# Top-10 indices of 8192 rows: the end of the kernel overlapped by hand, and one tile's loads divided by partitions

## The chip, the cores and the metric

One core of a Trainium2 chip. The metric is the device time of one execution in microseconds; a kernel's number is the median of its fast runs. How ratios are computed: the mean time of one kernel's fast runs over the mean of the other's fast runs of the same rounds, which is not quite the ratio of the medians quoted beside it.

## The reference

```python
def setup_inputs():
    return {"x": np.random.randn(8192, 8192).astype(np.float32), "k": 10}

def reference(x, k):
    indices = np.argpartition(x, -k, axis=1)[:, -k:]
    values = np.take_along_axis(x, indices, axis=1)
    sorted_idx = np.argsort(-values, axis=1)
    return np.take_along_axis(indices, sorted_idx, axis=1)
```

## The kernel before

The 268 MB of x pass the core once, in 64 tiles of 128 rows (4.2 MB each). A tile goes through these stages: SP issues its loads (four pieces); ScalarE takes exp(36(x - 4.7)) in bf16; PE sums groups of these with a 0/1 matrix, so that large elements stand out (1024 sums per row group, 512 for the last three "thin" tiles); VectorE chooses the 12 largest sums and their indices; GpSimd (POOL) gathers the candidates from the tile; VectorE and POOL spread them by a mask; PE extracts them; VectorE ranks them. Every eight tiles or so a batch is finished and written. At the end a check decides whether a slow fallback must run.

```python
    def load(t):
        lay = layout(t)
        xts[t] = xpool.tile([P, N], fp32, tag="xt", name="xt")          # 4 buffers
        src = x[t * P:(t + 1) * P, :].rearrange("(s a) (q j) -> (a q) s j", a=lay.A, q=lay.R)
        dst = xts[t].rearrange("p (s j) -> p s j", j=lay.W)
        n = lay.S // (8 if t in (0, last) else 4)
        for s in range(0, lay.S, n):
            nc.sync.dma_start(out=dst[:, s:s + n, :], in_=src[:, s:s + n, :])
    ...                                                # (cut)
    with tc.manual_schedule():
        weigh(0)
        later = []
        for t in range(last):
            interleave(choose_steps(t), rank_steps(t - LAG) if t >= LAG else [])
            if t >= 1:
                spread(t - 1)
            gather(t)
            weigh(t + 1)
            ...                                        # (cut: extract, steps of a finished batch)
            if t + 3 < ntiles:
                load(t + 3)
        extract(last - 3)
        extract(last - 2)
        run(choose_steps(last))
        spread(last - 1)
        gather(last)
        extract(last - 1)
        ...                                            # (cut: check, rankings, two batches)
```

## Time and profile before

| | before |
|---|---|
| median time | 683.44 us (682.9 to 683.74, 3 runs) |
| span of the profiled run | 679.8 us |
| transfer rate in the loop | about 420 GB/s |
| VectorE, PE, ScalarE, POOL busy | 82%, 81%, 72%, 26% |

The way to read it: the DMA share is 9 tenths in 38 of 40 slices, so the kernel is bound by them, and what a change of the end can win lies behind the last landing. The prediction below shows the lines and reads them.

### The profile page before, as it was taken

How to read it: one execution, taken by the hardware profiler on the slowest of the kernel's cores; microseconds unless marked ns; L12 is line 12 of the kernel's file. 1: busy time of each engine (PE TensorE's matmuls, PEld its weight loads, DVE VectorE, ACT ScalarE, POOL GpSimd, SP SyncE). 2: the span in 40 equal slices, each digit the busy share in tenths (PEclk: the TensorE clock that was granted, in tenths of full speed). 3: DMA queues.
4: the chain of work that ended last, by engine and by line, in shares of the span. 5: the costliest groups of instructions: out<-in, count | busy, mean ns of one | idle time of the engine just before them, and what ended most of it. 6: DMA issues, size and time to landing. Idle time of an engine off the chain costs nothing.

```text
span 679.8 us, 7988 instructions
## 1 busy us (share of the span) xinstructions
PE 549.6 (81%) x2690; PEld 339.5 (50%) x2690; DVE 555.5 (82%) x1335; ACT 488.7 (72%) x264; POOL 178.9 (26%) x134
## 2 busy tenths in 40 slices
PE   1577777888887889887987898898888789887887
PEld 0144544554544565553753555655454355454566
DVE  2577878699779978789796998879977889879687
ACT  4777777777777777777777777777777777777740
POOL 0113133313322322313322313322332231331330
PEclk9887887687878768597686768767788768778786
DMA  9999999999999999999999999999999999999910
GB/s 351 420 421 420 422 418 419 421 419 421 420 420 420 421 419 420 421 419 421 420 421 419 421 419 422 418 420 421 419 421 419 421 419 419 420 420 392 385 39 7
DMA packets 73696, 269.77 MB, mean 397 GB/s; under 512 B 4382, under 2 KB 5046, under 8 KB 73654
## 3 DMA queue, kind: packets, MB, share of 16 engines
q1 hardware_dynamic: 72960, 268.54, 96.8%
q10 hardware_dynamic: 694, 0.71, 0.3%
q8 instruction: 21, 0.34, 0.2%
q14 instruction: 21, 0.17, 0.1%
HBM read 268.58 MB, written 0.66 MB: 396 GB/s over the span
## 4 chain that ended last, share of the span: by engine, by line
DMA 62%; PE 10%; DVE 8%; SPq 6%; ACT 5%; issue 4%; POOL 3%; ACTq 0%; DVEq 0%
DMA xt<-in_x_dram 62%; PE s L169 8%; SPq L101 6%; ACT e L162 5%; POOL cand L203 3%; PE g L233 2%; DVE wall L189 2%; DVE m L190 1%; DVE masked L221 1%; DVE cidb L194 0%; DVE cidb L192 0%; DVE wall L193 0%; DVE rows L301 0%; DVE g L246 0%; DVE pick L298 0%
## 5 line engine op out<-in xcount | busy, mean ns | idle before, releaser
L162 ACT ACTIVATE e<-xt,bias 128x4096 bf16<-128x4096 f32 (+2 forms) x131 | 475.5, 3630 | 155.4 <-DMA xt<-in_x_dram 143.2
L169 PE MATMUL s<-e,group 128*128 128x512 bf16 x1024 | 337.5, 491 | 123.7 <-ACT e L162 123.4
L169 PEld LDWEIGHTS <-group 128*128 128x128 bf16 x1024 | 121.7, 122 | 316.3 <-issue 259.4
L233 PEld LDWEIGHTS g<-cpack,masked 128*128 128x128 f32 x1536 | 206.4, 214 | 16.5 <-issue 5.4
L233 PE MATMUL g<-cpack,masked 128*128 128x8 f32 (+1 forms) x1536 | 199.1, 269 | 1.7 <-DVE masked L221 1.7
L203 POOL INDIRECT_COPY cand<-xt,idx 128x192 f32 x64 | 64.9, 1014 | 478.8 <-DMA xt<-in_x_dram 181.8
L189 DVE MAX8 wall<-s 128x8 f32<-128x1024 f32 (+1 forms) x64 | 77.2, 1206 | 116.2 <-PE s L169 116.1
L221 POOL TENSOR_TENSOR masked<-cand,cpack 128x768 f32<-128x768 f32 x63 | 113.1, 1795 | 5.3
L192 DVE FIND_INDEX8 cidb<-wall,s 128x8 uint16<-128x1024 f32 (+1 forms) x64 | 76.6, 1197 | 0.0
L194 DVE FIND_INDEX8 cidb<-wall,m 128x8 uint16<-128x1024 f32 (+1 forms) x64 | 76.3, 1193 | 0.0
L190 DVE MATCH_REPLACE8 m<-wall,s 128x1024 f32<-128x1024 f32 (+1 forms) x64 | 76.0, 1188 | 0.0
L193 DVE MAX8 wall<-m 128x8 f32<-128x1024 f32 (+1 forms) x64 | 75.6, 1181 | 0.0
L221 DVE TENSOR_TENSOR masked<-cand,cpack 128x768 f32<-128x768 f32 x64 | 61.4, 960 | 0.9 <-POOL cand L203 0.9
L281 PE MATMUL fo<-rows,send 128*64 128x160 f32 (+3 forms) x128 | 27.9, 369 | 1.1 <-DVE rows L301 1.1
L162 ACT ACTIVATION_READ_ACCUMULATOR e<-xt,bias 128x1 f32 x131 | 24.4, 186 | 0.0
L281 PEld LDWEIGHTS fo<-rows,send 128*64 128x64 f32 (+2 forms) x128 | 18.3, 159 | 3.5 <-DVE rows L301 1.6
L248 DVE FIND_INDEX8 posb<-t8a,g 128x8 uint16<-128x96 f32 (+1 forms) x64 | 16.6, 260 | 0.0
L250 DVE FIND_INDEX8 posb<-t8b,g 128x8 uint16<-128x96 f32 (+1 forms) x64 | 16.4, 255 | 0.0
L245 DVE MAX8 t8a<-g 128x8 f32<-128x96 f32 (+1 forms) x64 | 16.1, 252 | 0.0
L246 DVE MATCH_REPLACE8 g<-t8a,g 128x96 f32<-128x96 f32 (+1 forms) x64 | 16.1, 251 | 0.0
L249 DVE MAX8 t8b<-g 128x8 f32<-128x96 f32 (+1 forms) x64 | 15.8, 246 | 0.0
L362 ACT ACTIVATE e<-tall,bias 128x64 f32<-128x64 f32 x1 | 0.3, 347 | 19.6 <-DVE tall L251 19.6
(37 smaller groups left out, 105.7 us busy)
## 6 DMA issues: line engine op xcount, KB each, us to landing
xt<-in_x_dram SPq DMA_DIRECT2D x248, 1024.0 KB, 16.3
xt<-in_x_dram SPq DMA_DIRECT2D x16, 512.0 KB, 9.4
out_dram<-opack ACTq DMA_DIRECT2D x6, 80.0 KB, 5.2
cpack<-topk_cpack ACTq DMA_DIRECT2D x1, 141.0 KB, 3.3
out_dram<-opack ACTq DMA_DIRECT2D x1, 70.0 KB
out_dram<-opack SPq DMA_DIRECT2D x1, 60.0 KB, 1.9
out_dram<-opack SPq DMA_DIRECT2D x1, 30.0 KB, 1.5
```

What stands on the lines that cost most here:

```text
L101: nc.sync.dma_start(out=dst[:, s:s + n, :], in_=src[:, s:s + n, :])
L162: nc.scalar.activation(out=e[:, 0:n * W], in_=xts[t][:, s0 * W:(s0 + n) * W], func=ACTF.Exp, bias=bias[:, 0:1], scale=BETA, accum_out=eall ...
L169: nc.tensor.matmul(ss[t][:, j:j + BANK], lhsT=lay.group[:, s0 + i, :], rhs=e[:, i * W + j:i * W + j + BANK], start=s0 + i == 0, stop=s0 + ...
L189: lambda: nc.vector.max(out=w16[:, 0:8], in_=m),
L190: lambda: nc.vector.match_replace(out=m2, in_to_replace=w16[:, 0:8], in_values=m, imm_value=-1.0),
L192: lambda: nc.vector.max_index(out=cid[:, 0:8], in_max=w16[:, 0:8], in_values=m),
L193: lambda: nc.vector.max(out=w16[:, 8:16], in_=m2),
L194: lambda: nc.vector.max_index(out=cid[:, 8:16], in_max=w16[:, 8:16], in_values=m2),
L203: nc.gpsimd.add_instruction(mybir.InstIndirectCopy(name=nc.get_next_instruction_name(), ins=[nc.gpsimd.lower_ap(xts[t]), nc.gpsimd.lower_a ...
L221: eng.tensor_tensor(out=masked[t][:, g0:g1], in0=cand[:, g0:g1].unsqueeze(2).to_broadcast(shape), in1=layout(t).own.rearrange("p (c s) -> ...
L233: nc.tensor.matmul(gs[t][:, c * R:(c + 1) * R], lhsT=mk[:, c, :, :].rearrange("p a s -> p (a s)"), rhs=layout(t).place, start=True, stop=True)
L281: nc.tensor.matmul(fo, lhsT=lay.send[:, i, 0:n * S], rhs=rows[:, i].rearrange("p a k -> p (a k)"), start=i == 0, stop=i == n - 1)
```

## The change

Two intents. The first is to overlap the last three tiles by hand: finer pieces for ScalarE and PE, the last two gathers in two halves, work of one tile put between the steps of another, some work of the last but one batch moved from VectorE to ScalarE. The second is to divide the loads of tile 61 by partitions, so that the DMA engines thought to run late get less. (Late: of the 16 semaphore increments that the trace of before shows for a load, one comes 2.5 to 2.9 us after the next in the last dozen loads. That one, or the DMA engine behind it, is called the straggler.) The pad is meant to keep the tiles' addresses at the same place modulo 512 bytes.

```diff
-PAD = 208
+PAD = 320
+
+DIVIDED = [[120, P], [120, 124, P], [112, P], [104, P]]
...
-        n = lay.S // (8 if t in (0, last) else 4)
-        for s in range(0, lay.S, n):
-            nc.sync.dma_start(out=dst[:, s:s + n, :], in_=src[:, s:s + n, :])
+        s = 0
+        for i, n in enumerate(pieces(t)):
+            bounds = DIVIDED[i] if t == last - 2 else [P]
+            for p0, p1 in zip([0] + bounds, bounds):
+                nc.sync.dma_start(out=dst[p0:p1, s:s + n, :], in_=src[p0:p1, s:s + n, :])
+            s += n
...
+        a, b, c = last - 2, last - 1, last
+        run(later)
+        wb, wc = weigh_steps(b), weigh_steps(c)
+        run(wb[0:3])
+        extract(a - 1, 0, 6)
+        run(wb[3:4])
+        extract(a - 1, 6, G)
+        run(wc[0:4])
+        run(rank_steps(a - 2))
+        mask(nc.gpsimd, a, G // 2, G)
+        run(choose_steps(b))
...   (cut: the rest of the hand-made order; gather in halves; two steps on ScalarE)
```

More of the change, by code (lines that the diff above doesn't have):

```diff
@@ L92, in layout, with pieces, parts @@
         return thin if t >= ntiles - TAIL else wide
+    def pieces(t):
+        S = layout(t).S
+        if t == 0:
+            return [S // 8] * 8
+        return [S // 8] * 7 + [S // 16] * 2 if t == last else [S // 4] * 4
+    def parts(t):
+        S = layout(t).S
+        if t < ntiles - TAIL:
+            return [S // 2] * 2
+        return [S // 4] + [S // 8] * 5 + [S // 16] * 2 if t == last else [S // 4] * 4
     def load(t):
@@ L146 @@
     tall = consts.tile([P, ntiles], fp32)
-    nsums = 2 * ntiles + 3
+    first_sum = np.cumsum([0] + [len(parts(t)) for t in range(ntiles)]).tolist()
+    nsums = first_sum[-1]
     eall = consts.tile([P, nsums], fp32)
@@ L152, with weigh_steps @@
         nc.gpsimd.memset(o, 0)
-    def weigh(t):
+    def weigh_steps(t):
         lay = layout(t)
@@ L157, in weigh, with part @@
         ss[t] = spsum.tile([P, wide.W], fp32, tag="s", name="s")[:, 0:W]
-        parts = [S // 4, S // 4, S // 4, S // 8, S // 8] if t == last else [S // 2, S // 2]
-        s0 = 0
-        for h, n in enumerate(parts):
+        def part(h, s0, n):
             e = epool.tile([P, N // 2], bf16, tag="e", name="e")
@@ L164, in weigh @@
                 func=ACTF.Exp, bias=bias[:, 0:1], scale=BETA,
-                accum_out=eall[:, 2 * t + h:2 * t + h + 1],
+                accum_out=eall[:, first_sum[t] + h:first_sum[t] + h + 1],
             )
@@ L168, in weigh @@
                 for j in range(0, W, BANK):
-                    nc.tensor.matmul(ss[t][:, j:j + BANK], lhsT=lay.group[:, s0 + i, :],
+                    nc.tensor.matmul(sums[:, j:j + BANK], lhsT=lay.group[:, s0 + i, :],
                                      rhs=e[:, i * W + j:i * W + j + BANK],
                                      start=s0 + i == 0, stop=s0 + i == S - 1)
+        sums, steps, s0 = ss[t], [], 0
+        for h, n in enumerate(parts(t)):
+            steps.append(lambda h=h, s0=s0, n=n: part(h, s0, n))
             s0 += n
+        return steps
     def choose_steps(t):
@@ L187, in choose_steps, with index, gather @@
         idxs[t] = small.tile([P, G], u16, tag="idx", name="idx")
+        def index(g0, g1):
+            nc.vector.tensor_scalar(
+                out=idxs[t][:, g0:g1], in0=cid[:, g0:g1], scalar1=float(lay.W - 1),
+                scalar2=lay.base, op0=ALU.min, op1=ALU.add,
+            )
+        early = t >= last - 1
         return [
             lambda: nc.vector.max(out=w16[:, 0:8], in_=m),
+            lambda: nc.vector.max_index(out=cid[:, 0:8], in_max=w16[:, 0:8], in_values=m),
+        ] + ([lambda: index(0, G // 2), lambda: gather(t, 0, G // 2)] if early else []) + [
             lambda: nc.vector.match_replace(out=m2, in_to_replace=w16[:, 0:8], in_values=m,
                                             imm_value=-1.0),
-            lambda: nc.vector.max_index(out=cid[:, 0:8], in_max=w16[:, 0:8], in_values=m),
             lambda: nc.vector.max(out=w16[:, 8:16], in_=m2),
             lambda: nc.vector.max_index(out=cid[:, 8:16], in_max=w16[:, 8:16], in_values=m2),
-            lambda: nc.vector.tensor_scalar(
-                out=idxs[t], in0=cid[:, 0:G], scalar1=float(lay.W - 1), scalar2=lay.base,
-                op0=ALU.min, op1=ALU.add,
-            ),
-        ]
-    def gather(t):
-        cands[t] = small.tile([P, G, 16], fp32, tag="cand", name="cand")
+        ] + ([lambda: index(G // 2, G), lambda: gather(t, G // 2, G)] if early
+             else [lambda: index(0, G)])
+    def gather(t, g0, g1):
+        if g0 == 0:
+            cands[t] = small.tile([P, G, 16], fp32, tag="cand", name="cand")
         nc.gpsimd.add_instruction(
@@ L205, in gather @@
                 name=nc.get_next_instruction_name(),
-                ins=[nc.gpsimd.lower_ap(xts[t]), nc.gpsimd.lower_ap(idxs[t])],
-                outs=[nc.gpsimd.lower_ap(cands[t].rearrange("p g s -> p (g s)"))],
-                num_valid_indices=16 * G,
-            )
-        )
-        del xts[t], idxs[t]
-    def spread(t, ndve=G // 2):
-        masked[t] = small.tile([P, G, P // 16, 16], fp32, tag="masked", name="masked")
-        cand = cands.pop(t)
-        for eng, g0, g1 in ((nc.vector, 0, ndve), (nc.gpsimd, ndve, G)):
-            if g0 == g1:
-                continue
-            shape = [P, g1 - g0, P // 16, 16]
-            eng.tensor_tensor(
-                out=masked[t][:, g0:g1],
-                in0=cand[:, g0:g1].unsqueeze(2).to_broadcast(shape),
-                in1=layout(t).own.rearrange("p (c s) -> p c s", s=16).unsqueeze(1).to_broadcast(shape),
-                op=ALU.mult,
-            )
@@ L228, in extract, with mask @@
-    def extract(t):
-        mk = masked.pop(t)
-        gs[t] = gpsum.tile([P, G * thin.R], fp32, tag="g", name="g")
+                ins=[nc.gpsimd.lower_ap(xts[t]), nc.gpsimd.lower_ap(idxs[t][:, g0:g1])],
+                outs=[nc.gpsimd.lower_ap(cands[t][:, g0:g1].rearrange("p g s -> p (g s)"))],
+                num_valid_indices=16 * (g1 - g0),
+            )
+        )
+        if g1 == G:
+            del xts[t], idxs[t]
+    def mask(eng, t, g0, g1):
+        if t not in masked:
+            masked[t] = small.tile([P, G, P // 16, 16], fp32, tag="masked", name="masked")
+        if g0 == g1:
+            return
+        shape = [P, g1 - g0, P // 16, 16]
+        eng.tensor_tensor(
+            out=masked[t][:, g0:g1],
+            in0=cands[t][:, g0:g1].unsqueeze(2).to_broadcast(shape),
+            in1=layout(t).own.rearrange("p (c s) -> p c s", s=16).unsqueeze(1).to_broadcast(shape),
+            op=ALU.mult,
+        )
@@ L231, in extract, with spread @@
+    def spread(t):
+        mask(nc.vector, t, 0, G // 2)
+        mask(nc.gpsimd, t, G // 2, G)
+    def extract(t, c0=0, c1=G):
+        if c0 == 0:
+            gs[t] = gpsum.tile([P, G * thin.R], fp32, tag="g", name="g")
         R = layout(t).R
-        for c in range(G):
-            nc.tensor.matmul(gs[t][:, c * R:(c + 1) * R], lhsT=mk[:, c, :, :].rearrange("p a s -> p (a s)"),
+        for c in range(c0, c1):
+            nc.tensor.matmul(gs[t][:, c * R:(c + 1) * R],
+                             lhsT=masked[t][:, c, :, :].rearrange("p a s -> p (a s)"),
@@ L278, in finish_steps, with spread_rows, copy_out @@
         rshape = [P, n, A, KMAX]
+        def spread_rows():
+            if b != len(starts) - 2:
+                return nc.vector.tensor_tensor(
+                    out=rows, in0=val.unsqueeze(2).to_broadcast(rshape),
+                    in1=lay.own_a.unsqueeze(1).unsqueeze(3).to_broadcast(rshape), op=ALU.mult)
+            for a in range(A):
+                nc.scalar.activation(out=rows[:, :, a, :], in_=val, func=ACTF.Copy,
+                                     scale=lay.own_a[:, a:a + 1])
+        def copy_out():
+            res, src = o[:, :, :, 0], fo.rearrange("p (a k) -> p a k", k=KMAX)
+            if b != len(starts) - 2:
+                nc.vector.tensor_copy(out=res, in_=src)
+            else:
+                nc.scalar.copy(out=res, in_=src)
         def move(i):
@@ L300, in finish_steps @@
                 out=val, in0=low, scalar=float(W), in1=pick, op0=ALU.mult, op1=ALU.add),
-            lambda: nc.vector.tensor_tensor(
-                out=rows, in0=val.unsqueeze(2).to_broadcast(rshape),
-                in1=lay.own_a.unsqueeze(1).unsqueeze(3).to_broadcast(rshape), op=ALU.mult),
+            spread_rows,
         ] + [lambda i=i: move(i) for i in range(n)] + [
-            lambda: nc.vector.tensor_copy(
-                out=o[:, :, :, 0], in_=fo.rearrange("p (a k) -> p a k", k=KMAX)),
+            copy_out,
             lambda: queue.dma_start(out=out_rows[r0:r0 + n * S, :],
@@ L322 @@
     with tc.manual_schedule():
-        weigh(0)
+        run(weigh_steps(0))
         later = []
-        for t in range(last):
+        for t in range(last - 1):
             interleave(choose_steps(t), rank_steps(t - LAG) if t >= LAG else [])
@@ L328 @@
                 spread(t - 1)
-            gather(t)
-            weigh(t + 1)
+            gather(t, 0, G)
+            if t < last - 2:
+                run(weigh_steps(t + 1))
             if 1 <= t < last - 2:
@@ L340 @@
                 load(t + 3)
-        extract(last - 3)
-        extract(last - 2)
-        run(choose_steps(last))
-        spread(last - 1)
-        gather(last)
-        extract(last - 1)
+        a, b, c = last - 2, last - 1, last
[9 more added lines that the diff above has]
+        run(choose_steps(b))
+        mask(nc.vector, a, 0, G // 2)
+        extract(a, 0, 2)
+        run(wc[4:5])
+        extract(a, 2, 4)
+        run(wc[5:])
+        extract(a, 4, G)
+        run(rank_steps(a - 1))
+        steps = finish_steps(batch_of[a - 1])
+        run(steps[:4])
+        mask(nc.gpsimd, b, G // 2, G)
+        chosen = choose_steps(c)
+        run(chosen[:4])
+        mask(nc.vector, b, 0, G // 2)
+        run(chosen[4:])
+        extract(b)
+        run(steps[4:7])
+        mask(nc.vector, c, 0, G // 2)
+        extract(c, 0, G // 2)
         nc.vector.tensor_scalar(
@@ L349 @@
         )
-        run(rank_steps(last - 3))
-        run(rank_steps(last - 2))
-        steps = finish_steps(batch_of[last - 3])
-        run(steps[:2])
-        spread(last, G)
-        run(steps[2:7])
-        extract(last)
-        run(steps[7:-2])
-        run(rank_steps(last - 1))
-        run(rank_steps(last))
+        run(rank_steps(a))
+        mask(nc.vector, c, G // 2, G)
+        extract(c, G // 2, G)
+        run(steps[7:])
+        run(rank_steps(b))
+        run(rank_steps(c))
         nc.scalar.activation(out=e10, in_=tall, func=ACTF.Exp, bias=bias[:, 0:1], scale=BETA)
         final = finish_steps(batch_of[last])
-        run(final[:-2])
-        run(steps[-2:])
-        run(final[-2:])
+        run(final)
         nc.vector.scalar_tensor_tensor(
```

## The prediction

> **What bounds the kernel now.** I read the page first (busy shares, the 40 slices, the chain that ended last), then the time of the engines and of the transfers in two-microsecond windows over the last 60 us, and then the timeline from 636 us on, row by row. From the page:
>
> ```profile
> PE 549.6 (81%) x2690; PEld 339.5 (50%) x2690; DVE 555.5 (82%) x1335; ACT 488.7 (72%) x264; POOL 178.9 (26%) x134
> ...
> DMA  9999999999999999999999999999999999999910
> GB/s 351 420 421 420 422 418 419 421 419 421 420 420 420 421 419 420 421 419 421 420 421 419 421 419 422 418 420 421 419 421 419 421 419 419 420 420 392 385 39 7
> ...
> DMA 62%; PE 10%; DVE 8%; SPq 6%; ACT 5%; issue 4%; POOL 3%; ACTq 0%; DVEq 0%
> ```
>
> No engine is the bound: the transfers are, at about 420 GB/s in 35 of 40 slices. 268.54 MB at 420 GB/s are 639 us of the span of 679.8. What is not transfer is a start of a few us and the last two slices (of 17 us each), where the rate falls to 39 and 7 GB/s. Only the end can give something, so the rest is about 636 to 680 us. The windows there (columns: PE, weight loads, DVE, ACT, POOL busy; granted clock; DMA share; GB/s):
>
> ```profile
> 638.00:640.00 2.00, 1.39 (x14) 1.31 (x14) 2.00 (x9) 1.93 (x2) 1.50 (x2) 1.00 1.04 395
> 640.00:642.00 2.00, 2.00 (x6) 0.77 (x6) 2.00 (x9) 0.78 (x1) 1.32 (x1) 0.60 0.97 375
> 642.00:644.00 2.00, 1.16 (x3) 0.30 (x2) 0.27 (x1) 2.00 (x1) 0.00 (x0) 0.54 0.88 291
> 644.00:646.00 2.00, 0.93 (x5) 0.45 (x5) 0.00 (x0) 2.00 (x3) 0.36 (x1) 1.00 0.98 377
> 646.00:648.00 2.00, 1.90 (x9) 0.71 (x8) 1.00 (x4) 2.00 (x3) 1.92 (x2) 1.00 0.67 258
> 648.00:650.00 2.00, 1.04 (x5) 0.39 (x4) 2.00 (x8) 2.00 (x3) 0.28 (x1) 1.00 0.08 30
> 650.00:652.00 2.00, 1.00 (x5) 0.39 (x4) 2.00 (x9) 2.00 (x4) 0.00 (x0) 1.00 0.03 13
> ```
>
> At 420 GB/s one of 16 DMA engines moves 26 GB/s. So the 30 and 13 GB/s after 648 us are one engine working alone: it finishes about 3 us after the others. The semaphore landings in the trace say the same: the last transfer has 15 of its 16 increments by 648.7 us and the last at 651.4. Each of the dozen transfers before has the same straggler, 2.5 to 3 us behind the next.
>
> The timeline from there, the rows that carry the tail:
>
> ```profile
> 641.22 3.71 ACT L162 ACTIVATE e<-xt,bias 128x4096 bf16<-128x4096 f32 x1 [1.29 <-DMA xt<-in_x_dram]
> 647.00 0.70 DVE L189 MAX8 wall<-s 128x8 f32<-128x512 f32 x1 [4.73 <-PE s L169]
> 653.96 0.70 DVE L189 MAX8 wall<-s 128x8 f32<-128x512 f32 x1 [1.61 <-PE s L169]
> 657.54 0.84 DVE L195 TENSOR_SCALAR idx<-cidb,cpack 128x12 uint16<-128x12 uint16 x1
> 662.65 0.97 POOL L203 INDIRECT_COPY cand<-xt,idx 128x192 f32 x1 [4.29 <-DVE t8b L249]
> 663.66 1.76 DVE L221 TENSOR_TENSOR masked<-cand,cpack 128x1536 f32<-128x1536 f32 x1 [0.88 <-POOL cand L203]
> 668.03 1.16 DVE L301 TENSOR_TENSOR rows<-val,cpack 128x960 f32<-128x960 f32 x1
> 672.75 0.14 DVE L251 COPY tall<-t8b 128x1 f32<-128x1 f32 x1
> 677.16 0.15 DVE L377 CAST ngood<-gps 1x1 int32<-1x1 f32 x1 [0.37 <-PE gps L375]
> ```
>
> The second half of tile 62 is complete at 641.2, ScalarE takes 3.7 us for it, and VectorE stands for 4.73 us until its sums are there. Then it stands 1.61 us for the sums of tile 63. From 653.96 on VectorE is busy almost without a gap to 677.31, with one wait of 0.88 us for the last gather. So the end is set by the transfers to about 647 us and by VectorE's list of work after that.
>
> [...]the 56-partition output of 635.3 us has 14 increments that come with its data. [...]The trace has 1.98 to 2.00 us for 2048 elements and 1.13 for 1024[...]. [...]the index TENSOR_SCALAR at 657.54 took 0.84 us, where it takes 0.21 in the loop, and ended as the POOL multiply (656.82 to 658.37) did.[...]
>
> **The change part by part.**
> Divided loads of tile 61 (2 KB rows, 64 KB per engine and piece). [...]In the last piece of tile 62 the arrivals are, in order, mostly about 635.5, then 636.6, 637.3, 637.3, 638.2 and 641.1. [...]Five more issues at about 0.4 us of SP, spread over 12 us, cost nothing.
> Finer parts. Tile 62 in quarters: its last quarter lands at about 637.5 and its exponential takes 2.0 us, so ScalarE is done by 639.7 in place of 644.9. Tile 63 in eight parts ends 0.7 us (512 elements, an estimate from 1.13 and 1.98) after the last landing, 649 to 650 in place of 653.2.
> PE order. It ends tile 61's sums at 636.7 as before (it is held there by the moves to 632.8, not by data), then extracts until 639.4, 12 matmuls at 0.24 us to 642.3, half an extract (1.4), 4 more: tile 62's sums at about 644.9 (647.0 before). Then half an extract, 10 matmuls, tile 61's extract in thirds and the last 6: tile 63's sums at about 653 (653.9 before). So most of the earlier landing is lost behind PE's and VectorE's order.
> VectorE's list from 636.8 us, durations from the timeline: tile 61's choice with a ranking and its multiply 5.4; ranking 1.35; tile 62's choice with one more index step 4.0; multiply 0.95; ranking 1.35; four steps of the batch 1.65; tile 63's choice 4.0; multiply 0.95; reduction and combination 1.15; multiply 0.95; check 0.15; ranking 1.85; multiply 0.95; two rankings 3.7; and from there to the end as before, 672.83 to 677.31, 4.48. Sum 32.9: the list would end at 669.7 without a wait, 7.6 earlier. Taken off VectorE: the 1.16 of rows and the copy, which go to ScalarE, idle for 19.6 us there. There 16 activations of 60 elements at about 0.33 us minus overlap are some 4 us, ready before PE needs them.
> Waits added back. For tile 62's sums: VectorE is free at 643.6, so 1.3. For the gathers: the record shows 0.97 to 1.02 us, but it begins 4.29 us after the index step in most tiles (3.63 in the first), so a gather occupies some 4.7 to 5.3 us. If the halves take half, about 2.4 and 0.9 more for a VectorE multiply that collides, then POOL runs: multiply to 648.5, two gathers of tile 62 to about 656, multiply to 658, first gather of tile 63 to 660.7, second to about 664. VectorE meets this with some 2 us of waiting. Sum 1.3 + 2 to 2.5: end of the list at about 673.2, gain 4.1. The pad grows by 448 bytes, which with the larger sums tables makes about 512 bytes of shift: kept alignment, no time.
>
> **The rivals.** (a) The gather is a fixed cost, not per index. Then four half gathers are about 19 us in POOL's queue, which has two multiplies more to do: the last gather would end near 669 and the kernel at about 683, no gain. For it: the 4.29 us is the same for rows of 1024 and 512. Against it: that would hold for a cost per index too, and the wait grows by 0.6 to 1.4 us when a VectorE multiply runs in it[...]. (b) The transfers are the path to the end, so that an earlier landing (3.4 us) is gained on top: 675 to 676. Against it: PE's order puts six pieces of other work before the last sums. (c) PE falls behind: it was granted a clock of 0.54 to 0.60 from 640 to 644, where a matmul takes 0.43. If that meets 16 matmuls of the tail, tile 63's sums come 1 to 3 us later: 680 to 682.
>
> **Range and chances.** 683.44 - 4.1 is 679.3, with the weights of (a) and (c) somewhat above that of (b). 8 in 10: 676.6 to 682.4. A change of 2% is 13.7 us, more than the whole 7.6 of VectorE's list, so faster by over 2% has 0.01; slower by over 2% would need a hurt steady state (the shifted buffers, the odd partition counts), 0.01; within 2% 0.98.
>
> **What would show it.** Landings: GB/s near 380 up to 647 and then 0, without two windows at one engine's rate. VectorE's wait for tile 62's sums about 1 us, not 4.73; tile 63's first MAX8 at 652 to 654, hardly earlier than before. Half gathers about 0.5 us in the record and 2 to 3 us after their index steps; if 4.3, (a) is right. The chain at the end on VectorE and POOL. I am wrong if the 420 GB/s of the loop moves, if tile 63's sums start well before 652, or if the list from there is not near 23 us.

The sum came to 4.1 us of gain (7.6 us of VectorE's list, less waits of 1.3 and of 2 to 2.5 us). The landing of tile 62's last quarter at about 637.5 us, and the end of tile 63 at 649 to 650 in place of 653.2 (a landing 3.4 us earlier), stand as estimates, without their ground. 1.98 to 2.00 and 1.13 us are ScalarE's exponentials. Measured beside two other terms: the 16 activations of 60 elements took 0.328 to 0.345 us each in the changed kernel, for the 0.33 expected; and the wait before a gather's record in before was 3.63 us in the first tile, with no mask multiply of VectorE in it, and 4.2 to 5.7 us in the others, with one.

## The result, and the profile after

The changed kernel took 694.56 us (694.23 to 696.25, 4 runs) against 683.28 us (4 runs, the three above and one more): ratio 1.017, interval 1.0152 to 1.0187. It is 11.3 us slower, where 4.1 us of gain were predicted and 682.4 us was the upper end of the range. The page of the changed kernel:

```profile
DMA  9999999999999999999999999999999999999920
GB/s 355 420 421 420 419 421 419 420 420 421 420 421 419 419 421 419 421 419 421 420 420 420 419 420 420 420 420 421 419 420 421 420 419 419 420 307 224 321 92 7
...
DMA 68%; PE 10%; SPq 6%; ACT 4%; issue 4%; DVE 4%; POOL 3%; ACTq 0%; DVEq 0%
```

The two rows, one above the other, show the finding. The transfer engines are as busy as before (9 tenths in 38 slices), but in slices 36 to 38 they move 307, 224 and 321 GB/s, where before had 420, 392 and 385. The steady loop has not changed. In windows of 4 us, before first (columns: PE, weight loads, DVE, ACT, POOL busy; granted clock; DMA share; GB/s):

```profile
612.00:616.00 4.00, 2.80 (x17) 1.60 (x15) 4.00 (x12) 2.81 (x3) 0.00 (x0) 0.86 1.02 410
624.00:628.00 4.00, 4.00 (x20) 2.28 (x18) 4.00 (x8) 2.29 (x1) 0.00 (x0) 0.66 1.01 392
632.00:636.00 4.00, 4.00 (x18) 1.66 (x17) 3.28 (x10) 2.56 (x2) 1.39 (x1) 0.80 1.05 409
```

The same windows of the changed kernel, with one before and one after:

```profile
608.00:612.00 4.00, 4.00 (x19) 3.57 (x19) 4.00 (x9) 2.90 (x3) 2.22 (x2) 0.50 1.02 417
612.00:616.00 4.00, 4.00 (x13) 1.55 (x12) 3.96 (x12) 1.97 (x3) 0.00 (x0) 0.65 0.98 301
624.00:628.00 4.00, 0.00 (x0) 0.00 (x0) 2.89 (x7) 1.65 (x1) 0.00 (x0) 0.63 1.07 205
632.00:636.00 4.00, 4.00 (x18) 3.09 (x16) 2.19 (x4) 1.45 (x2) 1.16 (x1) 0.50 0.96 230
640.00:644.00 4.00, 4.00 (x18) 2.54 (x17) 2.15 (x7) 2.10 (x2) 0.00 (x0) 0.73 1.01 344
```

From 612 us, when most engines reach tile 61, the rate halves for some 26 us, at a DMA share that stays close to 1 (0.88 at the least, from 628 to 632 us). So for the most part the engines do not wait for issues; each packet takes longer. The trace's packets say so: a packet of 2048 bytes took 84 ns (median) at 612 to 614 us and 120 to 162 ns in the windows of 2 us from 614 to 640; packets of 4096 bytes of the tile before, still under way, went from 159 to over 280 ns. Between 610 and 640 us the changed kernel moved some 4.7 MB less than before, which at 420 GB/s is 11 us. By the end more is lost: the last increment of the last load lands at 667.0 us, where before had 651.4, which is 15.6 us later, and the overlap wins some 4 us of it back (experiments below). The straggler did not go away either: at the last load it came 4.4 us behind the other 15 increments (662.6 and 667.0), and 2.7 in before (648.7 and 651.4).

The end itself shows the overlap doing its work, only later (rows of the changed kernel's timeline):

```profile
662.22 0.70 DVE L223 MAX8 wall<-s 128x8 f32<-128x512 f32 x1 [4.74 <-PE s L189]
663.76 0.23 DVE L215 TENSOR_SCALAR idx<-cidb,cpack 128x6 uint16<-128x6 uint16 x1
665.62 0.94 POOL L236 INDIRECT_COPY cand<-xt,idx 128x96 f32 x1 [3.47 <-DVE wall L228]
670.25 0.69 DVE L223 MAX8 wall<-s 128x8 f32<-128x512 f32 x1
689.74 0.14 DVE L449 CAST ngood<-gps 1x1 int32<-1x1 f32 x1 [0.37 <-PE gps L447]
```

From tile 63's first step to the end it now takes 19.6 us (670.25 to 689.88), where before took 23.4 (653.96 to 677.31). The first half gather is done 2.6 us after its index step (663.99 to 666.56); the other three took 3.1 to 3.4 us, counted from the index step or from POOL's last work before it, and whole gathers of before 4.7 to 6.7, mostly 5.3.

### The profile page after: what moved, and what is told of

It reads as the page before. It is cut to its first block, busy times and chain, and to the rows that moved or that the text cites. A ratio compares the mean times of both kernels' runs of the same rounds, so it can differ in the third digit from the quotient of the medians.

```text
span 692.4 us, 8036 instructions
## 1 busy us (share of the span) xinstructions
PE 556.6 (80%) x2690; PEld 346.6 (50%) x2690; DVE 555.2 (80%) x1336; ACT 495.3 (72%) x295; POOL 181.0 (26%) x136
## 4 chain that ended last, share of the span: by engine, by line
DMA 68%; PE 10%; SPq 6%; ACT 4%; issue 4%; DVE 4%; POOL 3%; ACTq 0%; DVEq 0%
DMA xt<-in_x_dram 68%; PE s L189 6%; SPq L120 6%; ACT e L182 4%; PE g L270 4%; POOL cand L236 3%; DVE wall L223 1%; DVE cidb L224 0%; DVE masked L253 0%; DVE cidb L229 0%; DVE m L226 0%; DVE wall L228 0%; DVE hot L347 0%; DVE t8a L283 0%; DVE posb L288 0%
## 5 line engine op out<-in xcount | busy, mean ns | idle before, releaser
L189 PE MATMUL s<-e,group 128*128 128x512 bf16 x1024 | 342.2, 496 | 127.5 <-ACT e L182 127.2
L270 PEld LDWEIGHTS g<-cpack,masked 128*128 128x128 f32 x1536 | 214.2, 220 | 20.6 <-issue 10.6
L270 PE MATMUL g<-cpack,masked 128*128 128x8 f32 (+1 forms) x1536 | 205.2, 273 | 3.4 <-DVE masked L253 3.3
L236 POOL INDIRECT_COPY cand<-xt,idx 128x192 f32 (+1 forms) x66 | 66.7, 1011 | 491.6 <-DMA xt<-in_x_dram 225.1
L215 DVE TENSOR_SCALAR idx<-cidb,cpack 128x12 uint16<-128x12 uint16 (+1 forms) x66 | 14.1, 214 | 0.2
## 6 DMA issues: line engine op xcount, KB each, us to landing
xt<-in_x_dram SPq DMA_DIRECT2D x2, 960.0 KB, 23.4
```

Source lines behind the costliest of these rows:

```text
L189: nc.tensor.matmul(sums[:, j:j + BANK], lhsT=lay.group[:, s0 + i, :], rhs=e[:, i * W + j:i * W + j + BANK], start=s0 + i == 0, stop=s0 + i ...
L236: nc.gpsimd.add_instruction(mybir.InstIndirectCopy(name=nc.get_next_instruction_name(), ins=[nc.gpsimd.lower_ap(xts[t]), nc.gpsimd.lower_a ...
L270: nc.tensor.matmul(gs[t][:, c * R:(c + 1) * R], lhsT=masked[t][:, c, :, :].rearrange("p a s -> p (a s)"), rhs=layout(t).place, start=True, ...
```

## The experiments

The theories. **1a, the partitions:** which partitions a load takes decides whether it is fast or slow by itself; in a slow one every packet takes twice as long. **1b:** uneven or small loads as such are slow. **1c:** the order of the reads in HBM. **2:** the division relieves the wrong engine and burdens the straggler. **3:** nine loads run into the eight semaphores that the loads use in turn (eight in the landings of before), and the issue stalls. **4, the rival to all:** the new order of work holds up buffers and so the loads.

The gather of both kernels may not be run in an experiment, so a stand-in takes its place in all of these. Their indices are wrong.

```diff
-        nc.gpsimd.add_instruction(mybir.InstIndirectCopy(...))
+        nc.gpsimd.tensor_copy(out=cands[t][:, g0:g1, 0], in_=idxs[t][:, g0:g1])
+        for _ in range(BURN * (g1 - g0) // G):        # BURN = 4, 832 elements each
+            nc.gpsimd.memset(burn, 0.0)
+        nc.gpsimd.tensor_copy(out=cands[t][:, g0:g1].rearrange("p g s -> p (g s)"),
+                              in_=xts[t][:, 16 * g0:16 * g1])
...
-            out=good[...], in0=e10, scalar=SLACK, in1=wall[:, :, G], op0=ALU.mult, ...
+            out=good[...], in0=e10, scalar=1e30, in1=wall[:, :, G], op0=ALU.add, ...
```

**s_before**, the kernel before with the stand-in, nothing else.

> Control. The gather may not be sent to the chip in an experiment, so a stand-in takes its place in this and all further kernels: a small copy that waits for the index step, four fills of 832 elements on the same engine, and a copy of 192 elements out of the tile. The indices that come out are wrong on purpose, and the final comparison is opened so that the slow fallback does not run. If the stand-in takes about as long as the gather (4.7 to 5.3 us after the index step), this runs in 681 to 686 us, as the kernel before did (683.3).

683.63 us against 684.1 for the kernel before in the same rounds; ratio 1.0001 (0.9984 to 1.0018). The stand-in keeps the time.

**s_after**, the changed kernel with the stand-in.

> Control. The changed kernel with the same stand-in (half as many fills for a half gather). 692 to 697 us if the loss of 11.3 us has nothing to do with the real gather; near 683 if the gather in halves was its cause. The transfer rate should fall to 200 to 300 GB/s between 610 and 640 us again.

696.48 us, ratio 1.0192 (1.0172 to 1.0211), and 225 GB/s on average from 612 to 636 us. The loss is there without the real gather, so the gather in halves is not its cause.

**s_overlap**, the changed kernel with whole loads.

```diff
-DIVIDED = [[120, P], [120, 124, P], [112, P], [104, P]]
+DIVIDED = [[P], [P], [P], [P]]
```

> The changed kernel with tile 61 loaded in four whole pieces: only the overlap is left. Theory 1 (the divided loads are the whole loss, the overlap itself is a gain): 677 to 681 us, rate 390 GB/s or more until 647 us. Rival (the new order of work holds up the buffers and so the loads): 690 us or more, with the rate still falling.

680.06 us, ratio 0.9942 (0.9925 to 0.9958): 4.0 us faster than before. Theory 4 is out. In its timeline:

```profile
646.73 0.70 DVE L225 MAX8 wall<-s 128x8 f32<-128x512 f32 x1 [2.29 <-PE s L191]
654.44 1.76 DVE L349 TENSOR_TENSOR hot<-hot,cidb 128x720 f16<-128x720 f16 x1
656.12 0.69 DVE L225 MAX8 wall<-s 128x8 f32<-128x512 f32 x1
```

VectorE's wait for tile 62's sums is 2.29 us, not 4.73, and tile 63's first step comes even 2.2 us later than in before (656.12 to 653.96), and 1.3 later than in s_before (654.78). The gain is that more of the list is done by then: from that step to VectorE's last one it takes 20.1 us, in s_before 23.5.

**s_divided**, the kernel before with the divided loads alone.

```diff
-        for s in range(0, lay.S, n):
-            nc.sync.dma_start(out=dst[:, s:s + n, :], in_=src[:, s:s + n, :])
+        for i, s in enumerate(range(0, lay.S, n)):
+            bounds = DIVIDED[i] if t == last - 2 else [P]
+            for p0, p1 in zip([0] + bounds, bounds):
+                nc.sync.dma_start(out=dst[p0:p1, s:s + n, :], in_=src[p0:p1, s:s + n, :])
```

> The kernel before with nothing changed but the divided loads of tile 61. Theory 1: 693 to 698 us, rate halved for some 20 us from about 612 us on although the DMA share stays near 1. Rival (order of work): 682 to 685 us.

699.63 us, ratio 1.0239 (1.022 to 1.0259), 16 us slower: more than expected. The divided loads are the whole loss. The two parts add up: -4.0 + 16.3 is 12.3 us, and s_after lost 13.1 (1.92%), which the intervals allow.

**s_nine**, the stand-in kernel with tile 61 in nine loads of all partitions.

```diff
+        cuts = [0, 2, 4, 6, 8, 10, 12, 14, 15, 16] if t == last - 2 else list(range(0, lay.S + 1, n))
+        for s0, s1 in zip(cuts, cuts[1:]):
+            nc.sync.dma_start(out=dst[:, s0:s1, :], in_=src[:, s0:s1, :])
```

> The stand-in of the kernel before, with tile 61 in nine loads of all 128 partitions, cut along the rows. Theory 1a and theory 2: 682 to 685 us, as the number of loads is not the cause. Theory 3 (nine loads run into the eight semaphores and the issue stalls): 688 us or more.

684.07 us, ratio 1.0006 (0.999 to 1.0022). The number of loads costs nothing; theory 3 is out.

**s_halves**, the pieces of tile 61 as partitions 0 to 63 and 64 to 127.

```diff
+DIVIDED = [[64, P], [64, P], [64, P], [64, P]]      # as in s_divided
```

> The stand-in of the kernel before, with each piece of tile 61 loaded as partitions 0 to 63 and 64 to 127: [...]in eight loads. Theory 1a[...]: the rate halves for the four pieces, 4.2 MB at 210 in place of 410 GB/s, so 8 to 11 us slower, 692 to 695. Theory 2 (uneven shares, the wrong engine burdened) and theory 3 (too many loads for the semaphores): theory 2 says 683 to 685, theory 3 says slower as the nine loads are.

697.71 us, ratio 1.0209 (1.0195 to 1.0224), 14.3 us slower with loads of equal size. (Before's outputs of 64 partitions have 16 increments that come with data; that these loads give every engine equal bytes is an estimate from that.) Uneven loads are not needed for the loss, so theory 2 is not its main part. The size was over the 8 to 11 us that I expected.

**e_rates**, the loads by themselves (one look; groups of four or eight loads, each group after the one before).

```diff
+        for c, (kind, ranges) in enumerate(PROBES):       # kind: rows of 2 (thin), 4 (wide), 8 KB (row)
+            ...
+            for s in range(0, lay.S, lay.S // 4):
+                for p0, p1 in ranges:
+                    nc.sync.dma_start(out=dst[p0:p1, s:s + lay.S // 4, :], in_=src[p0:p1, s:s + lay.S // 4, :])
+            nc.vector.tensor_copy(out=pad[:, 16:32], in_=pt[:, ::512])    # waits for all of the group
```

> The disputed cost by itself: after the work of the stand-in kernel, 17 groups of loads into one tile, each group waiting for the one before, with the partitions divided in different ways; rates read from the transfer windows. Theory 1a[...]: all 128 partitions 390 to 420 GB/s; 0 to 63 near 210; 32 to 95[...], near 400; 120 + 8 near 210; the same whether rows of 2, 4 or 8 KB are read. Theory 1b (uneven shares or small loads as such): 0 to 63 and 32 to 95 alike, 64 + 64 as fast as 128, and 120 + 8 slow. Theory 1c (the order of the reads in HBM): the halving depends on the kind of row read.

The windows inside twelve of the 17 groups; no engine works, and the last two columns are DMA share and GB/s. In order: rows of 2 KB, all 128 partitions; 120 + 8; 112 + 16; 104 + 24; 64 + 64; 0 to 63 alone; 32 to 95 alone; 0 to 119 alone; rows of 4 KB, all; 120 + 8; 0 to 63; 32 to 95.

```profile
682.00:688.00 6.00, 0.00 (x0) 0.00 (x0) 0.00 (x0) 0.00 (x0) 0.00 (x0) 0.50 0.99 376
698.00:710.00 12.00, 0.00 (x0) 0.00 (x0) 0.00 (x0) 0.00 (x0) 0.00 (x0) 0.50 1.00 195
722.00:731.00 9.00, 0.00 (x0) 0.00 (x0) 0.00 (x0) 0.00 (x0) 0.00 (x0) 0.50 1.06 268
740.00:752.00 12.00, 0.00 (x0) 0.00 (x0) 0.00 (x0) 0.00 (x0) 0.00 (x0) 0.50 0.86 189
764.00:776.00 12.00, 0.00 (x0) 0.00 (x0) 0.00 (x0) 0.00 (x0) 0.00 (x0) 0.50 1.07 229
784.00:792.00 8.00, 0.00 (x0) 0.00 (x0) 0.00 (x0) 0.00 (x0) 0.00 (x0) 0.50 1.07 212
797.00:802.00 5.00, 0.00 (x0) 0.00 (x0) 0.00 (x0) 0.00 (x0) 0.00 (x0) 0.50 0.99 338
806.00:812.00 6.00, 0.00 (x0) 0.00 (x0) 0.00 (x0) 0.00 (x0) 0.00 (x0) 0.50 1.00 215
834.00:840.00 6.00, 0.00 (x0) 0.00 (x0) 0.00 (x0) 0.00 (x0) 0.00 (x0) 0.50 1.03 421
848.00:860.00 12.00, 0.00 (x0) 0.00 (x0) 0.00 (x0) 0.00 (x0) 0.00 (x0) 0.50 0.97 199
872.00:880.00 8.00, 0.00 (x0) 0.00 (x0) 0.00 (x0) 0.00 (x0) 0.00 (x0) 0.50 1.05 211
885.00:889.00 4.00, 0.00 (x0) 0.00 (x0) 0.00 (x0) 0.00 (x0) 0.00 (x0) 0.50 1.03 376
```

0 to 63 and 32 to 95 are loads of the same size, with the same number of partitions. One runs at 212, the other at 338 GB/s, with packets of 166 and 84 ns (medians over the groups). What differs is where the partitions lie (and, with them, which rows of x are read), so 1b is out as the cause of the halving. The load of 120 partitions is slow by itself, without the 8 behind it: 215 GB/s, packets of 161 ns. And 0 to 31 alone gave packets of 162 ns, like 0 to 63. Rows of 8 KB behaved alike (all 425, 120 + 8 208, 0 to 63 217, 32 to 95 356), so 1c has nothing for it. Theory 1a is left. Why some partitions are slow is in no trace, only the times of the packets.

**s_thirds**, tile 61's pieces as 32 to 95 (338 GB/s by itself, where all 128 ran at 376), 0 to 31 (packets of 162 ns by itself) and 96 to 127 (not timed by itself; that it is slow too was the author's estimate).

```diff
+        ranges = [(32, 96), (0, 32), (96, P)] if t == last - 2 else [(0, P)]
```

> The stand-in of the kernel before, each piece of tile 61 in three loads: partitions 32 to 95 ([...]full rate by itself), 0 to 31 and 96 to 127[...]. [...]there are twelve loads. Theory 1a[...]: only half of the bytes pass at half rate, 2.1 MB, so 5 to 8 us slower, 688 to 692. Rival (any division by partitions costs alike): 696 to 700, as the halves 0 to 63 and 64 to 127.

691.84 us, ratio 1.0134 (1.0108 to 1.0161), 9.2 us slower: well under the halves, a little over my 8.

**s_early**, the divided loads on tile 30 in place of tile 61.

```diff
-            bounds = DIVIDED[i] if t == last - 2 else [P]
+            bounds = DIVIDED[i] if t == 30 else [P]
```

> The stand-in of the kernel before, with the same divided loads put on tile 30, in the middle, in place of tile 61. If the cost is just the halved rate while the bytes of one tile pass (4.2 MB at about 205 in place of 420 GB/s, 10.3 us), it is lost anywhere: 692 to 696 us. If much of the 16 us belongs to the end (few buffers, the straggler's queue), it is 10 or less: under 694. Rival, the loop has slack and catches up: 684 to 687.

699.32 us, ratio 1.0234 (1.0217 to 1.0251): 16 us again, where I expected 10.3. It is not a matter of the end, and nothing is made up in the 33 tiles that follow. Its windows:

```profile
298.00:302.00 4.00, 2.38 (x11) 1.03 (x10) 3.99 (x9) 2.21 (x2) 2.51 (x4) 0.87 1.03 413
306.00:310.00 4.00, 3.42 (x8) 1.14 (x8) 4.00 (x12) 0.13 (x2) 0.65 (x1) 0.59 1.01 192
322.00:326.00 4.00, 0.00 (x0) 0.00 (x0) 4.00 (x12) 3.42 (x1) 0.00 (x0) 0.62 1.04 214
330.00:334.00 4.00, 0.00 (x0) 0.00 (x0) 0.00 (x0) 1.93 (x1) 3.62 (x4) 0.90 1.02 397
```

The slow stretch is some 25 us, too long for one tile's 4.2 MB at 205 GB/s (20.5 us). I counted the bytes of slow packets in the traces, those that took over 1.4 times the usual 84 ns (2 KB) or 159 ns (4 KB): 5.6 MB in s_early, 5.3 in s_divided, 5.4 in s_halves, 3.4 in s_thirds, and 0.5 in s_before, which is taken off. So some bytes of the tiles beside it, in flight at the same time, are slowed too (5.1, 4.9, 4.9 and 2.9 MB, where 4.2, 4.2, 4.2 and 2.1 were divided so as to be slow). An estimate: half rate for that many bytes costs once more their time at the full 420 or 405 GB/s, 12.1, 12.1, 12.1 and 7.2 us; measured were 16.0, 16.3, 14.3 and 9.2. Added up from the traces, the durations of all load packets, divided by 16 engines, grew by 14.7, 12.1, 11.6 and 6.5 us against s_before. That is the larger part of each. Of the other 1 to 4 us, about 1 us in s_divided and s_halves may be the straggler's, which ends the last load 4.6 and 4.4 us behind the others, and 3.4 in s_before. The rest was not taken apart and stays open; in s_thirds a part may be idle engines, as its DMA share fell to 0.64 from 624 to 628 us.

**e_engines**, which engine is late (one look): the overlap kernel with whole loads, and behind tile 61's loads tiny loads of 1, 2, 3, 4, 8 and 15 partitions.

```diff
+        if t == last - 2:
+            for j, n in enumerate([1, 2, 3, 4, 8, 15]):
+                nc.sync.dma_start(out=pad[0:n, 16 * j + 16:16 * j + 32], in_=x[0:n, 0:16])
```

> Which DMA engine is the straggler: the overlap kernel with tile 61 whole, and behind tile 61's loads six tiny loads of 1, 2, 3, 4, 8 and 15 partitions[...]. [...]the tiny load with 1, 2, 3 or 4 partitions shows from which number on one increment is 2 to 5 us late. About 680 to 684 us.

The semaphore landings in its trace (us from the span's start; the increments that came at once with the issue are left out):

```
1 partition:   626.5
2 partitions:  625.4 626.6
3 partitions:  625.6 625.6 626.8
4 partitions:  625.8 625.8 627.0 632.0
8 partitions:  625.8 626.0 626.0 626.0 626.1 627.2 627.5 632.2
15 partitions: most at 628.0 to 628.1, the last at 632.4
```

The late one comes in with the fourth partition, by 5.0 us (632.0 after 627.0); with one to three no increment is over 1.2 us behind the others. The changed kernel agrees: its load of partitions 120 to 123 has four increments, at 622.0, 623.4, 624.8 and 636.0 us, so there too a load of four partitions meets the straggler. Which engine that is, and whether the division gives it less or more, no trace shows. The kernel before was not tried.

**o_whole_gather**, the overlap with whole gathers for the last two tiles.

```diff
-        early = t >= last - 1
+        early = False
...
+        gather(b, 0, G)    # behind choose_steps(b);  gather(c, 0, G) behind tile 63's steps
```

> The overlap kernel without divided loads, and the gathers of the last two tiles whole, not in halves. Tile 63's masks must then wait for one gather of 4.5 us after the last index step: about 1 to 2 us of the overlap's 4.0 are lost, 681 to 682.5. If halving is worth nothing: 679.5 to 680.5.

681.45 us, ratio 0.997 (0.9951 to 0.9989). The halves seem to be worth some 1.9 us of the 4.0, but the two intervals overlap and the runs are from two chips, so only the direction agrees.

**o_later_batch**, the overlap with two steps of the finished batch behind tile 63's choice.

```diff
-        run(steps[:4])
+        run(steps[:2])
...
-        run(steps[4:7])
+        run(steps[2:7])
```

> The overlap kernel without divided loads, with two VectorE steps of the finished batch (0.91 and 1.76 us in its trace[...]) moved behind tile 63's choice. Tile 63's first step then starts when its sums are there, at about 654.5 in place of 656.1, and the two steps take 0.9 and 0.55 us: 0.5 to 1.5 us faster than the overlap kernel, 678.5 to 679.5. Rival: PE's extracts set the pace there and nothing is gained.

679.23 us, ratio 0.9939 (0.9922 to 0.9955).

```profile
654.26 0.70 DVE L225 MAX8 wall<-s 128x8 f32<-128x512 f32 x1 [0.86 <-PE s L191]
660.19 0.53 DVE L349 TENSOR_TENSOR hot<-hot,cidb 128x720 f16<-128x720 f16 x1
```

The two effects are there: the first step 1.9 us earlier, the multiply 0.53 in place of 1.76 us. The span is 677.5 us, 1.2 under the overlap kernel's; the ratios of the two, 0.9939 and 0.9942, do not tell them apart. Both beat the kernel before and, with the same stand-in, the changed kernel (s_after). As the real gather could not be run with them, this is shown for the stand-in only.

## Why the prediction was wrong

- **The step that failed** is the first of the part list, "Divided loads of tile 61". It took for granted that an engine keeps its 26 KB per us however the partitions are divided, so that only the bytes of each engine counted and the extra issues "cost nothing". The runs showed 16.3 us of loss from this step alone (s_divided), as the packets of such loads take up to twice as long (161 ns for 84 in the load of 120 partitions by itself). It was not among the three rivals. It appears only as "the odd partition counts" in the chance of being slower, at 0.01.
- **What takes its place.** The rate of a load of part of the partitions depends on which ones it takes. By themselves, 0 to 63 ran at 212 and 32 to 95 at 338 GB/s (211 and 376 with 4 KB rows); these two differ only in the partitions and the rows read, and three kinds of rows gave the same. 0 to 119 ran at 215, 120 + 8 at 195, 112 + 16 at 268 and 104 + 24 at 189, where all 128 had 376. Why these are slow was not shown, and which partitions an engine took is in no trace here: the measured rates say which of the tried divisions to avoid, and nothing of others.
- **Which engine is late** was a guess from the change's words, and nothing here shows that the division relieved it. The sign that it looked for, landings without one engine working alone, did not come: the last increment was 4.4 us behind at the last load.
- **The increments of the divided loads:** the load of 120 partitions has 15 that come with data, 104 has 13, 24 has 12.
- **The overlap was right, in sum, and partly by luck.** 4.1 us were predicted for both parts of the change together, 4.0 measured for the overlap alone, without the earlier landing on which the 4.1 counted. Its parts were off: tile 62's sums came at 646.7 and not 644.9, tile 63's first step at 656.1 and not about 653. The list from there on took about 20 us, as its own items say, and not the "near 23" of the last paragraph.
- **Rival (a) fell:** half a gather takes 2.6 to 3.4 us in the changed kernel, where a whole one takes 4.7 to 6.7. **Rival (b) was not put to the test:** the earlier landing that it needs never came (last increment at 667.0 us in the changed kernel, at 652.0 in s_overlap and 652.2 in s_before). **Rival (c)** was half right, in s_overlap: 12 matmuls of tile 62 took 4.44 us from 640.1 us on (0.37 each), where the prediction had 0.24 each although its own windows show a granted clock of 0.54 to 0.60 from 640 to 644 us. Tile 63's sums were there at 654.5 and not 653, without costing the gain.
- **"I am wrong if the 420 GB/s of the loop moves"**: it did not move in the loop, but in the place to which the change itself went.

## What to carry to other kernels

Before dividing a load by partitions, time such a load by itself: here two loads of 64 partitions ran at 212 and 338 GB/s, so equal size is no guarantee of the rate, and a single tile divided into slow loads cost 16 us at either of the two places tried. Look at GB/s and at the DMA share together: here a share of 1.07 at 205 GB/s (624 to 628 us of the changed kernel) went with packets of about 160 ns in place of 84, so the packets were slow, not the issues late. And find out from which partition on a late increment comes, with loads of 1, 2, 3 and 4 partitions, before moving work off an engine.
